# Sums of squares and spread roots of six token blocks as 512-column products, the small tiles' pool opened first, the last output tile in two halves

## The chip, the cores and the metric

The kernel runs on one core of one Trainium2 chip. The core has five engines that run their own instruction streams and wait for one another by semaphores: TensorE (PE in the profile; its weight loads are listed apart as PEld), VectorE (DVE), ScalarE (ACT), GpSimd (POOL) and SyncE (SP), which here issues nearly all DMAs. TensorE writes to PSUM, which has eight banks of 128 x 512 f32; the other tiles lie in SBUF. The metric is the device time of one execution in microseconds (us).

## What is computed

One layer of an encoder on two groups of tokens, 2048 and 512, each with 16 meta tokens in front. All is f32. Cut to what matters here:

```python
u = rms_norm(h, norm_g)                       # h: (tokens, 1024)
qa, ka, va, za, qb, kb, vb, zb, ga, gb = split(u @ w_in)
o_a = neighbourhood_attention(qa, ka, va)     # branch A
o_b = window_attention(qb, kb, vb)            # branch B
y_a = (o_a * silu(za)) @ w_proj_a
y_b = (o_b * silu(zb)) @ w_proj_b
h = h + (sigmoid(ga) * y_a + sigmoid(gb) * y_b) @ w_out
return rms_norm(h[meta tokens dropped], final_g)

def rms_norm(x, g):
    return x * rsqrt(mean(x * x, axis=-1) + 1e-6) * g
```

The two norms need, for every token, a sum of squares over 1024 features, its inverse root, and a multiplication of the token's features by that root.

## The kernel before

Activations lie feature-major: features on the 128 partitions, tokens along the free axis, in blocks (windows) of 512 tokens, numbered 0 to 4. A matrix product in f32 is done as three products of rounded parts: `h` is the value rounded to fp32r by a copy on ScalarE, `l` what is left, by a subtraction (`split`, L198 and L199 for weights); `mm3` (L144 to L146) does `wh*uh`, `wh*ul`, `wl*uh`, each with up to 512 columns.

**A sum of squares** is first added up elementwise over the eight feature tiles into one 128 x 512 tile of partial sums. What is left is a sum over the 128 partitions for each of 512 tokens, and the way back: a tile in which every partition holds the tokens' roots. Before the change, both use plain f32 products with 128-column pieces:

- `sums` (L168): for each of four pieces of 128 tokens, the piece is the stationary operand and a column of ones the moving one. The result is a 128 x 4 tile in PSUM, tokens on the partitions. The trace shows two instructions for each such product.
- `rsqrt` (L151 to L161) computes the inverse root on VectorE in small instructions: a shift and three Newton steps.
- `diagonal` (L175) multiplies `ident` by the roots: four 128 x 128 diagonal matrices side by side, 128 x 512.
- `spread` (L183): `ones` as stationary operand times each diagonal gives 128 x 512 in PSUM with every token's root on all partitions. A copy on ScalarE takes it to SBUF (`rbs` at L1346, `rsa` at L495).

**The order.** TensorE's order is written out by hand throughout, SyncE's in the first part and at the end; the order on the other engines is made by a scheduler that simulates the program with its own durations (`schedule_with_timeline_sim=True`). A group of steps is a generator, and `yield` marks where the next piece of other work goes.

**First part** (0 to about 740 us): projections. `pairs` does the products for two windows at once, 18 pairs of feature tiles with seven series of twelve products each, and calls `step(j, 0)`, `step(j, 1)` and `step(j, 2)` at three places of pair j. There one step of `ahead` runs, if (j, place) is in a list. In the first pass `ahead` is `prep_ahead`, which normalises windows 2 and 3 for the second pass: sixteen steps load x and add up squares (GpSimd, L472); then, at (9, 0), the sums, the roots and the diagonals (L477 on); at (9, 1) the loads of the first piece; at (10, 0) the spread (L495) and the scaling, and so on. The tiles are `x0` of pool `st`, with one buffer.

**Second part** (to about 1825 us): attention units of both branches, in which dense work is filled in: the remaining gate projections, then for each window `dense_pa` (products of branch A with `w_proj_a`, gates loaded into `sga`, L1294 multiplies them into `ta`), `dense_pb`, `dense_out` (products with `w_out`, residual, squares added up in `ssq` by GpSimd, L1336), and `dense_fin`, the final norm of windows 0 to 3. `dense_fin(w - 1)` runs beside `dense_pa(w)`: after every two sub-steps of products, one step of it. It issues sums, roots and the diagonals at its first step, and five steps later the spread, the copy `rbs`, and then eight multiplications of `hT` on GpSimd (L1350) with their stores. Its PSUM tiles come from `ps_d`, which has two banks and also serves the products of `dense_pa`. In this part GpSimd also does the low parts of the weights (L199).

`open_dense` closes the pools `uxp` (operands of window 4, small tiles) and `ev` (evictions) and opens in their memory first `mp` (products' results, `hT`) and then `dn` (small tiles: gate loads `sg` with three buffers, `ssq`, `rbs`, the roots).

**End**: `finish_end` does window 4 token-major: eight output tiles of 128 tokens x 512 features, (b, c) with c = 0 for all b first, 24 products of 512 columns each. Behind each: the residual is added (L1427), the square is summed along the free axis (L1428), and for c = 1 the root of the two sums is computed (L1432, L151 on) and both halves of the row are scaled (L1434, L1436) and stored.

Of the kernel before, what the change touches and what calls it, by code (L numbers as in the profile page):

```python
# [9 lines left out]
F32 = mybir.dt.float32  # L10
# [7 lines left out]
P = 128  # L18
# [77 lines left out]
def encoder_block(ctx: ExitStack, tc: tile.TileContext, xT, x_end, w_in, w_pa, w_pb, w_o, norm_g, final_g,  # L96
# [24 lines left out]

    const = ctx.enter_context(tc.tile_pool(name="const", bufs=1))
# [5 lines left out]
    nc.scalar.activation(warm, ones[:, 0:1], AF.Silu)  # L128
# [4 lines left out]

    def f32(ap):
        return ap.bitcast(F32)
# [28 lines left out]
    def sums(ssq, c0, m, nc_, psum, tag):  # L164

        v = psum.tile([P, WTOK], F32, tag=tag, name="fin_v")
        for c in range(nc_):
            nc.tensor.matmul(v[:m, c : c + 1], ssq[:, c0 + c * m : c0 + (c + 1) * m], ones[:, 0:1],  # L168
                             start=True, stop=True)
        return v[:m, :nc_]  # L170

# [7 lines left out]
    def spread(psum, tag, dg, m, nc_):  # L179

        rb = psum.tile([P, WTOK], F32, tag=tag, name="rs_rb")
        for c in range(nc_):
            nc.tensor.matmul(rb[:, c * P : c * P + m], ones[:m, :], dg[:m, c * m : c * m + m], start=True, stop=True)  # L183
        return rb
# [272 lines left out]
    def prep_ahead(w):  # L457
# [16 lines left out]
        v = ps_t.tile([P, WTOK], F32, tag="vt", name="fin_v")  # L474
        for i in range(2):
            for c in range(4):
                nc.tensor.matmul(v[:, 4 * i + c : 4 * i + c + 1], x0[:, i, c * P : (c + 1) * P], ones[:, 0:1],  # L477
                                 start=True, stop=True)
        r = rsqrt(uxp, v[:, :8], P, 8)
        dgs = [ev.tile([P, WTOK], F32, tag="t", name="rs_dg", bufs=3) for _ in range(2)]  # L480
        for i in range(2):
            diagonal(dgs[i], r[:, 4 * i : 4 * i + 4], P)
        yield
        for kk in range(4):
            x0 = st.tile([P, 4, WTOK], F32, tag="x0", name="xa", bufs=1)
            for half in range(2):
                move(x0[:, 2 * half : 2 * half + 2],
                     xT[(kk + 4 * half) * P : (kk + 4 * half + 1) * P, w * WTOK : (w + 2) * WTOK]
                     .rearrange("p (i t) -> p i t", t=WTOK))
            yield  # L490
            if kk == 0:
                rss = []
                for i in range(2):
                    rss.append(ev.tile([P, WTOK], F32, tag="t", name=f"rsa{i}", bufs=3))
                    nc.scalar.copy(rss[i], spread(ps_t, "vt", dgs[i], P, 4))  # L495
# [12 lines left out]
            move(pre_d[:, kk, 6], t4)  # L508
            yield
# [474 lines left out]
    steps = [(0, 1), *((n, i) for n in range(1, KT) for i in (0, 1)), (KT, 0), (9, 0), (9, 1),  # L984
# [284 lines left out]
    def open_dense():  # L1269
        last.close()  # L1270
        pools["m"] = ctx.enter_context(tc.tile_pool(name="mp", bufs=1, side="right", reuse_waits="tile"))
        pools["d"] = ctx.enter_context(tc.tile_pool(name="dn", bufs=2, side="right", reuse_waits="tile"))
# [83 lines left out]
    def finish_end():  # L1356
# [49 lines left out]
        def out(ps, b, c, ks):  # L1406
            wh, wl = halves[c]
            ts = slice(b * P, (b + 1) * P)
            for k in ks:
                mh, ml = ms[k]  # L1410
                nc.tensor.matmul(ps, mh[:, ts], wh[:, k, :], start=k == 0, stop=False)
                nc.tensor.matmul(ps, mh[:, ts], wl[:, k, :], start=False, stop=False)
                nc.tensor.matmul(ps, ml[:, ts], wh[:, k, :], start=False, stop=k == KT - 1)
# [5 lines left out]
        for c in range(2):  # L1419
            cs = slice(c * WTOK, (c + 1) * WTOK)  # L1420
            for b in range(4):
                ts = slice(b * P, (b + 1) * P)
                h, sq = hs[b], small[:, 4 * b : 4 * b + 3]
                ahead = bool(begun)
                ps = begun.pop(0) if ahead else bank("pse")
                out(ps, b, c, range(KT - 2 if ahead else 0, KT))
                nc.vector.tensor_add(h[:, cs], h[:, cs], ps)  # L1427
                nc.scalar.activation(ps, h[:, cs], AF.Square, accum_out=sq[:, c : c + 1])  # L1428
# [3 lines left out]
                nc.vector.tensor_add(sq[:, 2:3], sq[:, 0:1], sq[:, 1:2])  # L1432
                r = rsqrt(pools["d"], sq[:, 2:3], P, 1)
# [13 lines left out]
    def phases(w, br):  # L1447
# [208 lines left out]
```

## Time and profile before

| | us |
|---|---|
| median of three runs | 1897.26 |
| the three runs | 1896.54 to 1899.39 |
| the profiled execution | 1896.82 |
| its span, first to last instruction | 1894.7 |
| TensorE busy | 1863.0 |
| VectorE busy | 1341.5 |
| ScalarE busy | 1144.3 |
| GpSimd busy | 733.1 |

A row of the order of time reads: start, duration, engine, line, operation, output <- inputs, partitions x elements and types, number of merged instructions, and in brackets the idle time of the engine before it and what ended that. TensorE's products overlap: a row's duration is longer than the step from one start to the next, and it is the step that counts. A row of the waits reads: engine, output, line, what it waited for; us in total, number of times, the longest. A row of the groups ends with total busy time, mean ns of one, and the idle time before. A row of the windows gives the stretch and its length, then busy us and number of instructions of PE, PEld, DVE, ACT and POOL, then the granted clock, the share of the DMA engines, and GB/s. TensorE's granted clock was 0.999 in the mean over the span.

### The profile page before, as it was taken

Reading aid. Unit: us, or ns where it says so; the run is one execution under the profiler, and the core shown is the slowest. Engines: PE = TensorE matmul, PEld = TensorE weight load, DVE = VectorE, ACT = ScalarE, POOL = GpSimd, SP = SyncE. Lnnn points to the kernel's source line nnn. Section 1 sums busy time; section 2 is a strip of 40 time slices with the busy share of each in tenths; the row PEclk is TensorE's granted clock in tenths of the full one; section 3 lists DMA queues with packets and bytes.
Section 4 is the critical chain, followed back from the end, with each engine's and each line's share of the span. In section 5 each row is a group of like instructions: output and inputs, shape, how many; then the busy total and the mean of one; then the engine's idle time right before and its main releaser. Section 6 shows DMA issues by size and latency. Waiting matters only on the chain. (4 is left out here: it accounts for less than half of the span.)

```text
span 1894.7 us, 29723 instructions
## 1 busy us (share of the span) xinstructions
PE 1863.0 (98%) x9797; PEld 1585.1 (84%) x9797; DVE 1341.5 (71%) x2939; ACT 1144.3 (60%) x2523; POOL 733.1 (39%) x556
## 2 busy tenths in 40 slices
PE   8999999999999999999999999999999999999998
PEld 6898888888888888888888888888888888888886
DVE  8886666556477565444457888878888887888874
ACT  6454444444365444444456787897788778778932
POOL 2005442323102232323224336656754864585420
PEclk9999999999999999999999999999999999999999
DMA  7667756644296787644268878967976996697483
GB/s 262 236 177 293 209 173 183 212 172 178 84 354 227 218 222 199 201 135 160 106 218 306 264 230 264 305 201 254 314 246 216 290 313 212 213 315 253 125 289 141
DMA packets 290385, 424.83 MB, mean 224 GB/s; under 512 B 117416, under 2 KB 162040, under 8 KB 288696
## 3 DMA queue, kind: packets, MB, share of 16 engines
q1 hardware_dynamic: 289944, 422.93, 69.2%
q8 instruction: 78, 1.28, 0.3%
q14 instruction: 75, 0.61, 0.1%
q10 hardware_dynamic: 288, 0.01, 0.0%
HBM read 303.46 MB, written 119.39 MB: 223 GB/s over the span
## 5 line engine op out<-in xcount | busy, mean ns | idle before, releaser
L199 POOL TENSOR_TENSOR wt<-wraw,wt 128x512 fp32r<-128x512 f32 x164 | 215.0, 1328 | 283.9 <-ACT wt L198 283.9
L826 PE MATMUL pa<-u,wt 128*128 128x512 f32 x1008 | 242.7, 390 | 0.0
L826 PE MATMUL pa<-u,x 128*128 128x512 f32 x984 | 236.8, 389 | 0.9 <-ACT u L837 0.9
L198 ACT CAST wt<-wraw 128x512 fp32r<-128x512 f32 x312 | 177.7, 619 | 77.0 <-PE mm L146 36.4
L826 PEld LDWEIGHTS pa<-u,wt 128*128 128x128 f32 x1008 | 188.8, 188 | 39.1
L826 PEld LDWEIGHTS pa<-u,x 128*128 128x128 f32 x984 | 184.4, 188 | 40.1 <-ACT u L837 1.7
L797 POOL TENSOR_TENSOR s<-wraw,raw 128x512 f32<-128x512 f32 x40 | 58.3, 1457 | 275.1 <-DVE x L199 275.1
L144 PE MATMUL mm<-u,wt 128*128 128x512 f32 (+2 forms) x416 | 150.8, 362 | 8.0 <-ACT u L325 7.4
L792 POOL TENSOR_TENSOR s<-raw 128x512 f32<-128x512 f32 x40 | 58.4, 1461 | 253.5 <-DMA raw<-in_w_in_dram 250.1
L146 PE MATMUL mm<-u,wt 128*128 128x512 f32 (+2 forms) x416 | 147.1, 354 | 1.9 <-DVE wt L199 1.9
L145 PE MATMUL mm<-u,wt 128*128 128x512 f32 (+2 forms) x416 | 147.0, 353 | 0.7 <-DVE u L326 0.7
L199 DVE TENSOR_TENSOR wt<-wraw,wt 128x512 fp32r<-128x512 f32 x148 | 107.9, 767 | 53.2 <-ACT wt L198 52.8
L826 PE MATMUL pe<-u,wt 128*128 128x512 f32 x504 | 121.3, 390 | 0.0
L826 PE MATMUL pc<-u,wt 128*128 128x512 f32 x504 | 121.1, 389 | 0.0
L826 PE MATMUL pe<-u,x 128*128 128x512 f32 x480 | 115.3, 389 | 0.0
L826 PEld LDWEIGHTS pc<-u,wt 128*128 128x128 f32 x504 | 94.6, 188 | 19.6
L826 PEld LDWEIGHTS pe<-u,wt 128*128 128x128 f32 x504 | 94.5, 188 | 19.6
L1122 DVE TENSOR_TENSOR pl<-tp,ph 128x384 fp32r<-128x384 f32 (+6 forms) x160 | 94.5, 591 | 22.3 <-ACT ph L1121 20.6
L144 PE MATMUL pso<-mh,wt 128*128 128x512 f32 x256 | 107.1, 418 | 0.0
L805 POOL TENSOR_TENSOR s<-wraw,s 128x512 f32<-128x512 f32 x40 | 55.0, 1374 | 131.5 <-DVE wt L199 131.5
L826 PEld LDWEIGHTS pe<-u,x 128*128 128x128 f32 x480 | 90.1, 188 | 18.7
L1027 ACT ACTIVATE prs<-s,nm 128x402 f32<-128x402 f32 (+1 forms) x160 | 91.0, 571 | 20.8 <-DVE nm L1020 17.7
(246 smaller groups left out, 5028.0 us busy)
## 6 DMA issues: line engine op xcount, KB each, us to landing
wraw<-in_w_in_dram SPq DMA_DIRECT2D x86, 512.0 KB
qa<-evq SPq DMA_DIRECT2D x20, 1024.0 KB
raw<-in_w_in_dram SPq DMA_DIRECT2D x40, 512.0 KB
q<-qa SPq DMA_DIRECT2D x20, 1024.0 KB
wraw<-in_w_o_dram SPq DMA_DIRECT2D x32, 512.0 KB
kbt<-kb SPq DMA_DIRECT2D x32, 384.0 KB
qb<-evq SPq DMA_DIRECT2D x20, 512.0 KB
ka<-evk SPq DMA_DIRECT2D x20, 512.0 KB
```

What stands on the lines that cost most here:

```text
L144: nc.tensor.matmul(ps, wh, uh, start=first, stop=False)
L145: nc.tensor.matmul(ps, wh, ul, start=False, stop=False)
L146: nc.tensor.matmul(ps, wl, uh, start=False, stop=last)
L198: nc.scalar.copy(h, r)
L199: low[0] = (eng or lo_eng[0]).tensor_sub(l, r, f32(h)).ins
L792: eng.tensor_add(s1, a21, a22)
L797: eng.tensor_sub(s3, a11, a21)
L805: eng.tensor_sub(s4, a12, s2)
L826: nc.tensor.matmul(ps, wt[:, a, s], u[:, b, kk, :], start=first and kk == 0 and i == 0, stop=kk == 3 and i == 2, skip_group_check=True)
L1027: nc.scalar.activation(out, s, AF.Exp, bias=nm, scale=-1.0, accum_out=sm)
L1122: nc.vector.tensor_sub(pl_[:kb, a], tb, f32(ph_[:kb, a]))
```

## The change

- **Sums** of six token blocks, two in `prep_ahead` and four in `dense_fin`, are done by `sums_parts`: the tile of partial sums is split into two rounded parts, and `ones_r` (128 x 128, now fp32r) as stationary operand times each part, 512 columns, adds up to a 128 x 512 tile in PSUM in which every partition has all sums. Four multiplications of a 128 x 128 piece with `ident`, each with a reduction along the free axis, take out the diagonals: a 128 x 4 tile, as before.
- **The roots** are spread by `spread_parts`: roots are split into two parts, each gets its own diagonals (`diagonal_parts`), and two products of 512 columns add up in PSUM.
- In `prep_ahead` the steps move: the split at (8, 1), the sums and roots at (8, 2), now with four columns for each block instead of eight for both, the spread and the first loads at (9, 1); the diagonals lie in the `x0` buffer.
- In `dense_fin` the split is a step of its own, one step earlier than the sums, whose place in TensorE's order stays. The high part of the sums and of the diagonals use the buffer `rbs`, the low parts one of the three `sg` buffers and `ssq`.
- `open_dense` opens `dn` ahead of `mp`.
- The **last output tile** (3, 1) is done in two halves of 256 columns with a bank each; the residual and square of each half follow it.
- `ones` is made from `ident` by VectorE, and `warm` has its own memset. The two norms at the very beginning (`prep_last`, `prep_first`) keep their products.

```diff
-    ones = const.tile([P, P], F32, name="ones")
-    nc.vector.memset(ones, 1.0)
+    ones_r = const.tile([P, P], F32R, name="ones")
+    nc.vector.tensor_scalar(ones_r, ident, 0.0, 1.0, ALU.mult, ALU.add)
+    ones = f32(ones_r)
...
+    def sums_parts(small, h, l, psum, tag):
+        v = psum.tile([P, WTOK], F32, tag=tag, name="fin_v")
+        nc.tensor.matmul(v, ones_r, h, start=True, stop=False)
+        nc.tensor.matmul(v, ones_r, l, start=False, stop=True)
+        sq = small.tile([P, 8], F32, tag="rq0", name="rq")[:, :4]
+        for c in range(4):
+            piece = v[:, c * P : (c + 1) * P]
+            nc.vector.tensor_tensor_reduce(piece, piece, ident, 1.0, 0.0, ALU.mult, ALU.add, sq[:, c : c + 1])
+        return sq
+
+    def diagonal_parts(small, dh, dl, r):
+        rh, rl = (small.tile([P, 8], F32R, tag=f"rq{i}", name="rq")[:, :4] for i in (1, 2))
+        nc.scalar.copy(rh, r)
+        nc.vector.tensor_sub(rl, r, f32(rh))
+        diagonal(dh, f32(rh), P)
+        diagonal(dl, f32(rl), P)
+
+    def spread_parts(psum, tag, dh, dl):
+        rb = psum.tile([P, WTOK], F32, tag=tag, name="rs_rb")
+        nc.tensor.matmul(rb, ones_r, dh, start=True, stop=False)
+        nc.tensor.matmul(rb, ones_r, dl, start=False, stop=True)
+        return rb
...
     def prep_ahead(w):
...
+        parts = []
         for i in range(2):
-            for c in range(4):
-                nc.tensor.matmul(v[:, 4 * i + c : 4 * i + c + 1], x0[:, i, c * P : (c + 1) * P], ones[:, 0:1],
-                                 start=True, stop=True)
-        r = rsqrt(uxp, v[:, :8], P, 8)
-        dgs = [ev.tile([P, WTOK], F32, tag="t", name="rs_dg", bufs=3) for _ in range(2)]
+            e = ev.tile([P, 2, WTOK], F32R, tag="ev", name="xq")
+            split(e[:, 0, :], e[:, 1, :], x0[:, i])
+            parts.append((e[:, 0, :], e[:, 1, :]))
+        yield
+        dg = st.tile([P, 4, WTOK], F32R, tag="x0", name="rs_dg", bufs=1)
         for i in range(2):
-            diagonal(dgs[i], r[:, 4 * i : 4 * i + 4], P)
+            r = rsqrt(uxp, sums_parts(uxp, *parts[i], ps_t, "vt"), P, 4)
+            diagonal_parts(uxp, dg[:, i], dg[:, 2 + i], r)
         yield
+        rss = []
+        for i in range(2):
+            rss.append(ev.tile([P, WTOK], F32, tag="t", name=f"rsa{i}", bufs=3))
+            nc.scalar.copy(rss[i], spread_parts(ps_t, "vt", dg[:, i], dg[:, 2 + i]))
...
-    steps = [(0, 1), *((n, i) for n in range(1, KT) for i in (0, 1)), (KT, 0), (9, 0), (9, 1),
+    steps = [(0, 1), *((n, i) for n in range(1, KT) for i in (0, 1)), (KT, 0), (KT, 1), (KT, 2), (9, 1),
...
     def dense_fin(w):
-        r = rsqrt(pools["d"], sums(acc["s", w], 0, P, 4, ps_d, "d"), P, 4)
-        dg = pools["d"].tile([P, WTOK], F32, tag="rbs", name="rs_dg", bufs=1)
-        diagonal(dg, r, P)
+        small, ssq = pools["d"], acc["s", w]
+        sh = small.tile([P, WTOK], F32R, tag="rbs", name="ssh", bufs=1)
+        sl = small.tile([P, WTOK], F32R, tag="sg", name="ssl", bufs=3)
+        split(sh, sl, ssq)
+        yield
+        r = rsqrt(small, sums_parts(small, sh, sl, ps_d, "d"), P, 4)
+        dh, dl = (small.tile([P, WTOK], F32R, tag=t, name="rs_dg", bufs=1) for t in ("rbs", "ssq"))
+        diagonal_parts(small, dh, dl, r)
         for _ in range(5):
             yield
-        rb = spread(ps_d, "d", dg, P, 4)
+        rb = spread_parts(ps_d, "d", dh, dl)
...
+                if (b, c) == (3, 1):
+                    for i in range(2):
+                        x = slice(i * 2 * P, (i + 1) * 2 * P)
+                        ps = bank("pse")[:, : 2 * P]
+                        out(ps, b, c, range(KT), x)
+                        residual(ps, h[:, WTOK + x.start : WTOK + x.stop], sq[:, 1 + 2 * i : 2 + 2 * i])
...
-            yield from islice(pa, 3)
+            yield from islice(pa, 2)
             yield from with_fill(pa, dense_fin(w - 1))
```

More of the change, by code (lines that the diff above doesn't have):

```diff
@@ L120, in encoder_block, with f32 @@
     g_d = {(b, w, f): dt(f"g{b}{w}{f}", [P, WTOK]) for b in "ab" for w in range(NWIN) for f in range(KT)}
+    def f32(ap):
+        return ap.bitcast(F32)
     const = ctx.enter_context(tc.tile_pool(name="const", bufs=1))
@@ L162, in rsqrt @@
         return r
[L164 to L168, printed above, removed]
-                             start=True, stop=True)
-        return v[:m, :nc_]
     def diagonal(dg, r, m):
@@ L490, in prep_ahead @@
             yield
[L491 to L495, printed above, removed]
             x = [x0[:, j] for j in range(4)]
@@ L1270, in open_dense @@
         last.close()
-        pools["m"] = ctx.enter_context(tc.tile_pool(name="mp", bufs=1, side="right", reuse_waits="tile"))
-        pools["d"] = ctx.enter_context(tc.tile_pool(name="dn", bufs=2, side="right", reuse_waits="tile"))
+        for i, name, bufs in ("d", "dn", 2), ("m", "mp", 1):
+            pools[i] = ctx.enter_context(tc.tile_pool(name=name, bufs=bufs, side="right", reuse_waits="tile"))
     acc = {}
@@ L1405, in finish_end, with out @@
             move(hs[b], x_end[b * P : (b + 1) * P])
-        def out(ps, b, c, ks):
+        def out(ps, b, c, ks, x=slice(0, WTOK)):
             wh, wl = halves[c]
@@ L1422, in finish_end @@
                 ts = slice(b * P, (b + 1) * P)
-                h, sq = hs[b], small[:, 4 * b : 4 * b + 3]
+                h, sq = hs[b], small[:, 4 * b : 4 * b + 4]
                 ahead = bool(begun)
[L1425 to L1428, printed above, removed]
+                if (b, c) == (3, 1):
[4 more added lines that the diff above has]
+                        residual(ps, h[:, WTOK + x.start : WTOK + x.stop], sq[:, 1 + 2 * i : 2 + 2 * i])
+                        if i == 0:
+                            nc.vector.tensor_add(sq[:, 0:1], sq[:, 0:1], sq[:, 1:2])
+                    sq = sq[:, 0:4:3]
+                else:
+                    ps = begun.pop(0) if ahead else bank("pse")
+                    out(ps, b, c, range(KT - 2 if ahead else 0, KT))
+                    residual(ps, h[:, cs], sq[:, c : c + 1])
                 if c == 0:
@@ L1431, in finish_end @@
                     continue
-                nc.vector.tensor_add(sq[:, 2:3], sq[:, 0:1], sq[:, 1:2])
-                r = rsqrt(pools["d"], sq[:, 2:3], P, 1)
+                nc.vector.tensor_add(sq[:, 0:1], sq[:, 0:1], sq[:, 1:2])
+                r = rsqrt(pools["d"], sq[:, 0:1], P, 1)
                 nc.scalar.mul(h[:, :WTOK], h[:, :WTOK], r)
```

16 lines of the change are left out of this document (8 added, 8 removed).

## Prediction

> **What bounds the kernel now.** I read the page first, then who TensorE waited for, then the order of time around each place that the change touches.
>
> ```profile
> PE 1863.0 (98%) x9797; PEld 1585.1 (84%) x9797; DVE 1341.5 (71%) x2939; ACT 1144.3 (60%) x2523; POOL 733.1 (39%) x556
> PE psa L144 <- ACT rbs L1346: 2.5, 3, 0.9
> ```
>
> TensorE is busy nearly all of the span. So TensorE time that is removed is worth its full length, as long as no other engine is late at that place. The span is 1894.7 us in an execution of 1896.82 us, so 2.1 us lie around it; the median of the three runs is 1897.26 us, 0.44 above the profiled execution. I work against 1896.82.
>
> The second line is the wait that lies where the change does: three of the four blocks in the second half end with TensorE waiting up to 0.9 us for the copy `rbs` on ScalarE. What stands behind this wait decides the change.
>
> ```profile
> 1286.67 0.69 DVE L1294 TENSOR_TENSOR ta<-psa,sga 128x512 f32<-128x512 f32 x1
> 1287.42 0.50 PE L144 MATMUL psa<-ya,wt 128*128 128x512 f32 x1
> 1288.06 2.54 POOL L199 TENSOR_TENSOR wt<-wraw,wt 128x512 fp32r<-128x512 f32 x2 [6.26 <-ACT wt L198]
> 1288.24 1.14 DVE L152 TENSOR_SCALAR rs<-rs 128x4 int32<-128x4 int32 x1
> 1289.42 1.22 DVE L153 TENSOR_SCALAR rs<-rs 128x4 int32<-128x4 int32 x1
> 1295.56 0.68 DVE L175 TENSOR_TENSOR rs_dg<-ident,rs 128x512 f32<-128x512 f32 x1
> 1299.08 2.64 POOL L199 TENSOR_TENSOR wt<-wraw,wt 128x512 fp32r<-128x512 f32 x2 [8.48 <-ACT wt L198]
> 1300.08 1.05 PE L183 MATMUL rs_rb<-rs_dg,ones 128*128 128x128 f32 x8
> 1303.54 0.57 ACT L1346 COPY rbs<-rs_rb 128x512 f32<-128x512 f32 x1
> 1304.17 0.50 PE L144 MATMUL psa<-ya,wt 128*128 128x512 f32 x1 [0.88 <-ACT rbs L1346]
> 1292.00:1297.00 5.00, 5.00 (x34) 4.42 (x33) 4.89 (x19) 3.64 (x10) 0.00 (x0) 1.00 0.85 308
> ```
>
> These are rows in order of time of the first block, and one stretch of the windows (its third busy time is VectorE's). VectorE is full here: 4.89 of 5 us. Two tiny instructions of the root chain took 1.14 and 1.22 us, each until one of GpSimd's pair of subtractions was over. The copy `rbs` starts over 2 us after its products have ended, because ScalarE works through instructions that wait for VectorE. So in this block VectorE leads, and TensorE follows it at the end.
>
> **The change part by part. Products.** The old series of narrow products cost this much (last block; then the two blocks of `prep_ahead`):
>
> ```profile
> 1797.88 0.95 PE L168 MATMUL fin_v<-ones,ssq 128*128 128x1 f32 x8
> 1798.69 0.47 PE L144 MATMUL psa<-ya,wt 128*128 128x512 f32 x1
> 1799.01 0.39 PE L145 MATMUL psa<-ya,wt 128*128 128x512 f32 x1
> 1809.08 1.05 PE L183 MATMUL rs_rb<-rs_dg,ones 128*128 128x128 f32 x8
> 1809.88 0.48 PE L144 MATMUL psa<-ya,wt 128*128 128x512 f32 x1
> 291.67 2.88 PE L826 MATMUL pa<-u,x 128*128 128x512 f32 x12
> 294.39 1.84 PE L477 MATMUL fin_v<-ones,xa 128*128 128x1 f32 x16
> 298.95 2.88 PE L826 MATMUL pc<-u,wt 128*128 128x512 f32 x12
> 315.28 1.95 PE L183 MATMUL rs_rb<-rs_dg,ones 128*128 128x128 f32 x16
> 319.81 2.43 PE L826 MATMUL pc<-u,wt 128*128 128x512 f32 x10
> ```
>
> From 291.67 to 294.39 TensorE does twelve 512-column products: 2.72 us, 0.227 for one. In the last block the sums take 0.81 us up to the next product and that product 0.32 instead of 0.23: 0.90; the spread 0.80, and 0.09 behind it taken alike: 0.89; together 1.79. Four 512-column products take 4 x 0.227 = 0.91. That is 0.88 us of TensorE less in each of four `dense_fin`. In `prep_ahead`, from the sums to the next series but one are 4.56, and from the spread 4.53, each less 2.72: 1.84 + 1.81 = 3.65 for two blocks, against 8 x 0.227 = 1.82. That is 1.83 less. All six: 5.4 us.
>
> **What is added on the other engines.**
>
> ```profile
> L1020 DVE CUSTOM_DVE_ANT_0 s<-s,bb 128x274 f32<-128x274 f32 x32 | 13.8, 452 | 1.6 <-PE s L1201 1.2 <-ACT ph L1121 0.4
> L1020 DVE CUSTOM_DVE_ANT_0 s<-s,ba 128x512 f32<-128x512 f32 x32 | 21.9, 686 | 4.4 <-PE s L1092 4.3
> 300.81 0.17 DVE L159 TENSOR_TENSOR rs<-rs,rs 128x8 f32<-128x8 f32 x1
> ```
>
> A reduction of 128 columns isn't in the trace. The first two rows give 0.98 ns a column, so 0.31 us by their line; it is at most 0.45, with a small instruction of 0.17 to read its accumulator, and no less than such a small one. The last row shows one of these in the root chain; with the gap behind it I count 0.2 us a step. I take 0.3 for a reduction, four to a block: 1.2 us (0.7 to 2.5). A split costs VectorE about 0.69 (as `rs_dg`) and ScalarE about the 0.57 of `rbs`; the low part of the roots a small instruction of 0.17, the copy of the high part about 0.2 on ScalarE, and the second diagonal 0.69. Each block gets 2.7 us more of VectorE and 0.8 of ScalarE. In `dense_fin` the split is issued one step earlier and the rest where it was.
>
> *Blocks 1 to 3.* The split and the four reductions come before the two instructions that stood behind GpSimd until 1290.6 anyway; I count them as hidden by that wait (if GpSimd's pair comes elsewhere, they cost up to 1.8). But `psa` at 1287.42 follows within 0.06 us on the end of `ta` (1286.67 + 0.69), whose bank it takes; so the 0.45 saved on the sums is lost to this wait. Behind 1295.56 come 0.85 us (low part, second diagonal) on a full VectorE, ahead of what ScalarE needs before `rbs`. About half of that fits into VectorE's short idle times. So the wait for `rbs` ends 0.4 us later than now, wherever TensorE stands: +0.4 each, **+1.2** together. Bounds: -1.76 each (0.88 saved and the wait gone) to +2.7 each (all added VectorE time in the way).
>
> *Block 4 and `prep_ahead`.*
>
> ```profile
> 1810.83 7.67 POOL L1350 TENSOR_TENSOR hT<-hT,rbs 128x512 f32<-128x512 f32 x5 [17.76 <-ACT rbs L1346]
> 296.00:301.00 5.00, 5.00 (x25) 4.12 (x25) 4.87 (x11) 1.21 (x2) 2.60 (x2) 1.00 0.11 16
> 1280.53 1.27 POOL L1336 TENSOR_TENSOR ssq<-ssq,xres 128x512 f32<-128x512 f32 x1
> ```
>
> In the last block GpSimd stood idle for 17.8 us before `hT`, which follows on `rbs` less than 1 us after the spread; so nothing holds VectorE up and TensorE leads: **-0.9** (bounds -0.9 to +0.5, the low diagonal late).
>
> In `prep_ahead` the sums move to before the series at 291.67, the spread to before the third series behind the one at 298.95, about 307; so the chain has 14 us. It needs 2 x (1.2 + 13 steps of 0.2 + 0.5 for the copy's round trip + 0.17 + 1.3) = 11.5. VectorE has other work there, about 4.5 us by my estimate, and its window from 296 is full today. The second low diagonal comes about 0.7 us after TensorE asks for it: -1.83 + 0.7 = **-1.1** (-1.83 to +1.7 if all other work goes first). SyncE's loads at that step now wait for the spread too, since the diagonals stand in the loads' buffer; they are queued behind weight loads that wait for buffers, so I count nothing.
>
> *New waits.* The split on ScalarE waits for the last addition to `ssq`, which ends at 1281.8 in block 1, nearly 5 us ahead of the old sums, so the earlier step can have it. The copy of the high roots on ScalarE waits for the end of the root chain; behind it stand the attention units' exponentials, and TensorE's transposes wait for those. It costs nothing while the scheduler puts it late enough, and up to the chain's delay where it doesn't: that is in the bounds of +2.7. The low part of the sums takes one of the three `sg` buffers, so two gate loads go out a tile later; each still has two tiles of twelve products, over 5 us, and the load below took 3.8.
>
> **The pools' order.** The first gate load of the dense part lands late:
>
> ```profile
> 1118.80 0.41 SPq L140 DMA_DIRECT2D gb<-eva  x1
> 1122.09 6.41 SPq L140 DMA_DIRECT2D sga<-ga  x5
> 1125.93 0.69 DVE L1294 TENSOR_TENSOR ta<-psa,sga 128x512 f32<-128x512 f32 x1 [1.14 <-DMA sga<-ga]
> 1126.68 0.50 PE L144 MATMUL psa<-ya,wt 128*128 128x512 f32 x1 [0.57 <-DVE ta L1294]
> ```
>
> Now `dn` stands in memory that the evictions of the last gates used, so its first load can't start before `gb<-eva` has left; after the change it stands where the last window's operands were, free once the last gate's products are done. If the load goes 1 us earlier TensorE gets 0.57 back: **-0.6** (0 if SyncE's queue held it).
>
> **The last tile.**
>
> ```profile
> 64.93 0.28 PE L144 MATMUL mm<-u,wt 128*128 128x256 f32 x1
> 65.77 0.28 PE L145 MATMUL mm<-u,wt 128*128 128x256 f32 x1
> L1228 DVE TENSOR_TENSOR pl<-tp,ph 128x256 fp32r<-128x256 f32 x64 | 26.5, 414 | 0.0
> 1886.69 0.69 DVE L1427 TENSOR_TENSOR h<-h,pse 128x512 f32<-128x512 f32 x1 [1.04 <-PE pse L1413]
> 1887.47 0.60 ACT L1428 ACTIVATE pse<-h 128x512 f32<-128x512 f32 x1 [1.85 <-DVE h L1427]
> ```
>
> The first two are seven steps apart: 0.12 us for a 256-column product, so 48 x 0.12 = 5.76 against 24 x 0.227 = 5.44: +0.32 on the path. The tail is shorter by 0.11 (last product 0.28 instead of 0.39), 0.28 (addition 0.41 instead of 0.69) and about 0.22 (the square of 0.60, cut alike): **-0.3** in all. The first half's addition and square lie beside the second half's products. `ones` made from `ident` costs a fraction of a microsecond at a time when all engines still wait for the first loads: nothing.
>
> **Sum.** +1.2 - 0.9 - 1.1 - 0.6 - 0.3 = -1.7 us: 1895.1 on the profiled execution, **1895.5** beside the median.
>
> [...] One more row pair shows what the added instructions can meet:
>
> ```profile
> 298.57 1.30 POOL L793 TENSOR_TENSOR s<-s,wraw 128x512 f32<-128x512 f32 x1
> 298.76 1.14 DVE L159 TENSOR_TENSOR rs<-rs,rs 128x8 f32<-128x8 f32 x1
> ```
>
> An instruction of VectorE with two operands in SBUF, 0.17 us at 300.81, ended only when GpSimd's did. [...]
>
> **Rivals.**
>
> *All of it lands* (0.30). If the scheduler, which orders VectorE and ScalarE by its own simulated times, puts `rbs` ahead of the attention work, or the 0.85 us fit, nothing is given back: -(4 x 0.88 + 1.83 + 0.6 + 0.3) = -6.3, so 1891, and 1888.5 if the 2.5 us of waits for `rbs` go too. For it: TensorE is the bound at 98%. Against it: VectorE's 4.89 of 5 us.
>
> *The second diagonal meets GpSimd* (0.10; slower). The place is the pair of subtractions at 1299.08. The first diagonal now ends at 1296.2; with 0.85 us and the copy's round trip the second ends at 1297.5 to 1299. If it starts after 1299.08 it stands behind up to 2.64 us, the spread with it, and the maxima of the next attention units too; TensorE waits some 2.0 us more per block than now: 3 x 2.0, nothing won in block 4, +1.0 in `prep_ahead`, -0.9 for the rest: +6, so 1903. It decides from a chain that is 1.5 us longer than I take it.
>
> *The products are not cheaper* (0.05). If a 512-column product with the rounded `ones` cost as much as its four old pieces, only VectorE's work would be new: +1.2 + 0.4 + 0.7 - 0.9, so 1898.5.
>
> **How the numbers follow.** Forecast 0.55, between 1893 and 1898.5. About 0.2% (3.8 us) is what a measurement of this kernel can tell from no change. The case where all lands is over that line, with a small part of the forecast: faster 0.33. Slower 0.10, the second rival. Same 0.57. The range goes from 1889.5, most of the first rival, to 1900.5, which leaves out the second.
>
> **What would show it.** Right: `fin_v` and `rs_rb` with two products each, 0.45 us apart from the next; the wait for `rbs` still there in three blocks at about 1.3 us; none in the fourth; `sga` landing before `ta` asks; the tail from the last product to the end some 0.6 us shorter. Wrong: TensorE waiting for `rs_dg` in `dense_fin`, or the waits for `rbs` gone. What would overturn the sum is another order of VectorE's instructions over the whole second half, since the scheduler sees new durations.

## The result and the profile after

The change makes the kernel slower: median 1911.87 us, against 1898.41 us of the kernel before in all its runs up to then. The ratio is 1.0068, with a 95% interval from 1.0053 to 1.0083, so about 13 us. One of the six runs of the changed kernel took 5480.28 us, and one of the kernel before in a later batch 5386.77; ratios and intervals leave such runs out, and without it the median here is 1911.05. The prediction was 1895.5, in a range from 1889.5 to 1900.5.

The page of the changed kernel (its profiled execution took 1915.09 us, 4 us more than that median), then the waits of TensorE (engine and line, what it waited for, total, times, longest):

```profile
span 1912.9 us, 29727 instructions
PE 1874.3 (98%) x9749; PEld 1582.2 (83%) x9749; DVE 1355.1 (71%) x3021; ACT 1148.4 (60%) x2537; POOL 734.0 (38%) x556
```

```profile
PE tp L1140 <- DVE pr L1060: 5.4, 5, 2.4
PE rs_rb L204 <- DVE rs_dg L169: 5.2, 4, 1.7
PE rs_rb L205 <- DVE rs_dg L169: 2.4, 3, 1.1
PE psa L146 <- DVE ta L1316: 1.6, 3, 0.8
```

TensorE is busy for 11.3 us *more* than before (1863.0), though 5.4 us of its work were taken away. The waits on the new spreads (`rs_rb` for `rs_dg`) are 7.6 us; the 2.5 for `rbs` are gone. So waiting is not the whole story: something makes TensorE's own work longer. In the order of time, a stretch of the first part that the change doesn't touch:

```profile
618.55 2.88 PE L848 MATMUL pc<-u,wt 128*128 128x512 f32 x12
621.27 2.97 PE L848 MATMUL pa<-u,x 128*128 128x512 f32 x12
624.08 2.97 PE L848 MATMUL pe<-u,x 128*128 128x512 f32 x12
626.89 2.89 PE L848 MATMUL pa<-u,wt 128*128 128x512 f32 x12
629.62 2.88 PE L848 MATMUL pe<-u,wt 128*128 128x512 f32 x12
```

From start to start, the series at 618.55 and 626.89 take 2.72 and 2.73 us, as before. The two between them take 2.81: 0.234 us a product instead of 0.227. Of the seven series of a pair, these are the only two whose moving operand is `u[5]` or `u[6]`, the two operands that lie in the pool `uxp`.

The second place is `prep_ahead`'s spread, with a stretch of the windows behind it (after the six pairs of busy time and count: granted clock, DMA share, GB/s):

```profile
307.31 0.40 PE L204 MATMUL rs_rb<-rs_dg,ones 128*128 128x512 f32 x1
308.78 0.69 DVE L169 TENSOR_TENSOR rs_dg<-ident,rq 128x512 fp32r<-128x512 f32 x1
309.61 0.48 PE L204 MATMUL rs_rb<-rs_dg,ones 128*128 128x512 f32 x1 [1.68 <-DVE rs_dg L169]
309.99 0.68 DVE L169 TENSOR_TENSOR rs_dg<-ident,rq 128x512 fp32r<-128x512 f32 x1
310.72 0.50 PE L205 MATMUL rs_rb<-rs_dg,ones 128*128 128x512 f32 x1 [0.63 <-DVE rs_dg L169]
311.00:315.00 4.00, 4.00 (x12) 3.09 (x12) 1.47 (x3) 0.58 (x1) 1.66 (x1) 0.57 0.41 151
```

TensorE waits 2.3 us for the second block's diagonals. After that it is granted 0.57 of its clock for 4 us: the 12 products that start at 311.06 take 4.34 us up to the next series instead of 2.72. The granted clock is 0.50 from 311.43 to 314.84 us, so of these 3.41 us 1.7 are lost. Two more such stretches of 3.41 us follow: from 1536.82 us, behind a wait of 2.39 us for `pr`, and from 1826.95 us, behind the last `dense_fin`. In the profiled execution of the kernel before, the clock is 0.50 from 1890.94 us alone, behind the last product.

The third place is each `dense_fin`; the first block:

```profile
1296.94 0.40 PE L186 MATMUL fin_v<-ssl,ones 128*128 128x512 f32 x1
1298.16 0.50 PE L146 MATMUL psa<-ya,wt 128*128 128x512 f32 x1 [0.82 <-DVE ta L1316]
1308.57 3.08 POOL L221 TENSOR_TENSOR wt<-wraw,wt 128x512 fp32r<-128x512 f32 x2 [7.52 <-issue]
1309.07 1.45 DVE L1060 TENSOR_SCALAR pr<-pr,rd 128x384 f32<-128x384 f32 x1
1310.44 1.76 DVE L169 TENSOR_TENSOR rs_dg<-ident,rq 128x512 fp32r<-128x512 f32 x1
1312.25 0.50 PE L205 MATMUL rs_rb<-rs_dg,ones 128*128 128x512 f32 x1 [1.07 <-DVE rs_dg L169]
1313.32 0.57 ACT L1373 COPY rbs<-rs_rb 128x512 f32<-128x512 f32 x1
```

The sums are cheap, and TensorE then waits 0.82 us for `ta`. Ten microseconds later the second diagonal falls beside GpSimd's pair of subtractions (1308.57 to 1311.65) and takes 1.76 us instead of 0.69; TensorE waits for it. In the other blocks it is not the second diagonal. First the second block, then the last:

```profile
1480.41 2.65 POOL L221 TENSOR_TENSOR wt<-wraw,wt 128x512 fp32r<-128x512 f32 x2 [8.65 <-issue]
1481.85 1.23 DVE L197 TENSOR_TENSOR rq<-rs,rq 128x4 fp32r<-128x4 f32 x1
1483.73 0.50 PE L204 MATMUL rs_rb<-rs_dg,ones 128*128 128x512 f32 x1 [1.11 <-DVE rs_dg L169]
1825.24 0.49 PE L204 MATMUL rs_rb<-rs_dg,ones 128*128 128x512 f32 x1 [1.35 <-DVE rs_dg L169]
1826.45 0.50 PE L205 MATMUL rs_rb<-rs_dg,ones 128*128 128x512 f32 x1 [0.72 <-DVE rs_dg L169]
```

In the second block, and alike in the third, the low part of the roots (L197), which takes 0.16 us in the last block, lies beside GpSimd's pair and takes 1.23, so both diagonals come late. In the last block GpSimd stands still (19.87 us idle up to 1827.65); there the chain alone is too long. From the first reduction (1814.25) to the end of the high diagonal (1825.19) it takes 10.9 us with other work of VectorE in between; before the change, the roots and the diagonal took 6.0.

### The profile page after: what moved, and what is told of

Read it like the earlier page. It is cut to its first block, busy times and chain, and to the rows that moved or that the text cites. A ratio compares the mean times of both kernels' runs of the same rounds, so it can differ in the third digit from the quotient of the medians.

```text
span 1912.9 us, 29727 instructions
## 1 busy us (share of the span) xinstructions
PE 1874.3 (98%) x9749; PEld 1582.2 (83%) x9749; DVE 1355.1 (71%) x3021; ACT 1148.4 (60%) x2537; POOL 734.0 (38%) x556
## 5 line engine op out<-in xcount | busy, mean ns | idle before, releaser
L1143 ACT CAST ph<-tp 128x384 fp32r<-128x384 f32 (+6 forms) x160 | 81.2, 508 | 38.4 <-PE tp L1140 37.1
```

The source lines that it names most:

```text
L1143: nc.scalar.copy(ph_[:kb, a], tb)
```

## The experiments

Three theories: **place** (the new small tiles moved `u5` and `u6` in memory), **waits** (late diagonals, and the halved clock behind them), **order** (another order of VectorE, ScalarE and loads everywhere). Each time stands beside the median of the kernel before in the same batch of runs.

### Where the operands lie

e1, the kernel before with dead bytes, at the start of `prep_ahead`:

```diff
+        uxp.tile([P, 24], F32, tag="pad", name="pad")
```

> The kernel before, with nothing but 96 dead bytes per partition in the pool uxp, which moves u5, u6, u45 and u46 by the 96 bytes by which the change moves them. Theory 'place': a 512-column product takes 0.234 us instead of 0.227 when its moving operand and the weights that are loaded beside it start at different places within 128 bytes; 1008 products (pa, pe, pb and pg from x) would go from 0.227 to 0.234: about +7.1 us, up to +8.5 with the gates' products, so 1905 to 1907, and the series pa<-u,x at 2.81 us for twelve every second time. Theory 'order': the slower series of the changed kernel come from its other order of VectorE, ScalarE and the loads; then the padding alone changes nothing: 1898 and 2.72 us for twelve everywhere.

Measured: 1904.42 (before 1897.69; ratio 1.0037, 1.0025 to 1.0049): 6.7 us for 96 unused bytes.

```profile
500.78 2.97 PE L827 MATMUL pe<-u,x 128*128 128x512 f32 x12
503.59 2.89 PE L827 MATMUL pa<-u,wt 128*128 128x512 f32 x12
L827 PE MATMUL pe<-u,x 128*128 128x512 f32 x148 | 36.8, 396 | 0.0
```

Its instructions stand in the same order as before the change on every engine, and the series with `u6` takes 2.81 us (last row: the group between 330 and 640 us, with its mean of 396 ns). Place is shown; order falls for this part.

e2 moves the weights by 32 bytes as well; e3 is the changed kernel with 32 dead bytes more in `uxp` and 64 in `dn`:

```diff
     const = ctx.enter_context(tc.tile_pool(name="const", bufs=1))
+    const.tile([P, 8], F32, name="pad")            # e2, with e1's line
...
+        uxp.tile([P, 8], F32, tag="pad", name="pad")   # e3
...
+        pools["d"].tile([P, 16], F32, tag="pad", name="pad", bufs=1)   # e3
```

> The kernel before with those 96 bytes in uxp and 32 more in const, so that every operand of the first part, moving or weight, starts at a multiple of 128 bytes instead of 96 bytes behind one. If it is the difference of the two places that counts, the first part is back at 0.227 us a product and only the last output tiles (weights at 96, moving operand at 0) are slower, 0.233 for about 190 products: 1898 to 1900. If a start at a multiple of 128 is slow in itself, all 3500 products of the first part take 0.234: about +24 us, 1922. Theory 'order': 1898.

> The changed kernel with 32 dead bytes in uxp and 64 in dn, so that u5, u6, mh and ml start where they did before the change, within 128 bytes. 'Place': 1008 products get 0.007 us back, the gates' a little, and the 168 of the last output tiles 0.006 each: 7.1 + 1.1, so about -8 to -9 us, 1903 to 1904; what is left above the kernel before, some 5 us, is the waits for rs_dg and the halved clock behind them. 'Order': 1912, unchanged.

Measured: e2 1904.68 (1.0035, 1.0022 to 1.0048), e3 1909.46 (1.0069, 1.0054 to 1.0084). e2 misses all that was expected: the products with `u5` and `u6` are still slow, those with `u[0]` to `u[4]` fast, though all start at a multiple of 128. e3 brings next to nothing, as theory 'order' had it, but for another reason: its products with `u5` and `u6` are still slow too. From the start addresses in the built programs and the mean steps between starts of products (those under 0.26 us):

```
kernel        u5 starts at   weights x at   distance mod 256   step, u5 or u6 with x
before        190176         151008           0                0.227 us
changed, e1   190080         151008         160                0.234
e2            190080         151040         128                0.233
e3            190048         151008         128                0.233
f1 (below)    189920         151008           0                0.227
```

So in these kernels the step goes with the distance between the moving operand and the weights that are loaded beside it: 0.227 us where the last column but one is 0, 0.233 to 0.234 where it is 128 or 160. f1 moves `u5` and `u6` by 256 bytes against the kernel before:

```diff
+        uxp.tile([P, 40], F32, tag="pad", name="pad")
...
+        pools["d"].tile([P, 16], F32, tag="pad", name="pad", bufs=1)
```

> The changed kernel with 160 dead bytes in uxp and 64 in dn: u5, u6, u45 and u46 lie 256 bytes below where they lay before the change, so every moving operand and the weights loaded beside it start alike within 256 bytes, where the kernel with 32 dead bytes left them 128 apart. Theory 'place within 256': all products of the first part at 0.227 again, 1008 x 0.006 plus some 690 opening products x 0.004, so 7 to 8 us under the realigned kernel (1909.5): 1901 to 1903. Rival: the distance counts within 512 bytes or more, or the right-hand pool must lie exactly where it did; then 0.233 stays and the time is 1908 to 1910.

Measured: 1905.21 (before 1897.31; 1.0039, 1.0027 to 1.0051).

```profile
499.23 2.88 PE L849 MATMUL pe<-u,x 128*128 128x512 f32 x12
501.95 2.88 PE L849 MATMUL pa<-u,wt 128*128 128x512 f32 x12
L849 PE MATMUL pe<-u,x 128*128 128x512 f32 x158 | 38.1, 389 | 0.0
```

The products of the first part have their old step: the series at 499.23 takes 2.72 us, and one of `pe<-u,x` lasts 389 ns on the mean (last row, groups between 330 and 640 us), 396 in e1. The changed kernel stood 12.6 us over its runs of before (by the median of 1911.05), f1 7.9: 4.7 us by place here, with a margin of some 4 us, and 6.7 in e1. The two traces are sharper: f1's instructions stand in the same order as those of the changed kernel on every engine, and from 320 to 980 us the changed kernel falls 6.8 us behind it, step by step. The median is 2 to 4 us above what was expected, so more than the rest of the first part is left.

### Which of the parts costs the rest

e4 is the changed kernel with `prep_ahead` and its steps as before (`uxp` keeps its size by that) and 64 dead bytes in `dn`:

```diff
...
-    steps = [..., (KT, 0), (KT, 1), (KT, 2), (9, 1),
+    steps = [..., (KT, 0), (9, 0), (9, 1),
...
```

> The changed kernel with prep_ahead as before (its narrow products, one root for both blocks), so that uxp keeps its size, and 64 dead bytes in dn. Only dense_fin, the pools' order and the last tile differ from the kernel before. If the two waits for rs_dg at 309 us (1.7 and 0.6) and the halved clock behind them (3.4 us at half speed, so 1.7) cost 4.0 and the cheaper products give 1.8 back, this is 2 us faster than the realigned kernel: 1901 to 1902. If the second halves of the waits are hidden anyway, it is 1.8 slower than that: 1905.

Measured: 1898.26 (before 1897.69; 1.0002, 0.9994 to 1.0011). That is 7.3 us under f1, each beside its own runs of before; f1 differs in `prep_ahead` alone, and the distance is far more than the 2.3 us of its waits. (By the intervals given, a distance between two versions has a margin of 2 to 4 us.) And `dense_fin`, the pools and the tail together can't be told from nothing.

f2, f3 and f4 were to put the spread one step later, f3 in `dense_fin` too; f4 has the old `dense_fin`:

```diff
-    steps = [..., (KT, 0), (KT, 1), (KT, 2), (9, 1),
+    steps = [..., (KT, 0), (KT, 1), (9, 0), (9, 1),
...
-        for _ in range(5):      # f3, dense_fin
+        for _ in range(6):
```

> The same, and in prep_ahead the spread (and the loads behind it) one step later, where the loads stood before the change. Theory 'late diagonals': the waits for rs_dg at 309 us (1.7 + 0.6) go, and with them the 3.4 us at half clock behind them (1.7): about 4 us under the first of these, 1897 to 1899. Rival 'the scheduler moves it all back': VectorE's and ScalarE's instructions of the chain are issued later in the same measure and TensorE waits as long as before: 0.

> The same as f2, and in dense_fin the spread one step later too (six steps between diagonal and spread instead of five). Theory 'the low diagonal meets GpSimd and is late': the four waits for rs_dg (1.1 + 1.2 + 1.2 + 2.1 in the changed kernel) go, 5.5 us; where the copy rbs on ScalarE is then waited for again (0.9 in three blocks before), 3 are left: 3 to 5.5 us under f2, 1892 to 1895. Rival: rbs comes a step later too, hT with it, and the wait only changes its name: 0 to -1.

> f2 with dense_fin as before the change: narrow products, one diagonal, no split. It holds prep_ahead's products, the pools' order and the halved last tile alone. Expected against the kernel before: -1.8 for prep_ahead, -1.0 for the pools' order (the waits for ta and y at 1119 us gone), -0.5 at the tail, so 1894 to 1895. If dense_fin as changed is a loss (waits for rs_dg of 5.5 and for ta of 1.7, against 3.5 of products and 2.5 of old waits), this is 1 to 2 us under f2; if the two are even, 0.

Measured, against 1897.31: f2 1908.11 (1.0061, 1.0048 to 1.0074), f3 1915.06 (1.0093, 1.008 to 1.0106), f4 1904.4 (1.0038, 1.0026 to 1.005). All expectations missed, because the edit did something else: step (9, 0) runs the *sums*, so they came one series later and the spread stayed. That is the opposite test, and a clear one (f4):

```profile
307.63 0.40 PE L213 MATMUL rs_rb<-rs_dg,ones 128*128 128x512 f32 x1
313.18 0.76 PE L212 MATMUL rs_rb<-rs_dg,ones 128*128 128x512 f32 x1 [5.15 <-DVE rs_dg L169]
316.00:320.00 4.00, 4.00 (x14) 3.15 (x13) 0.00 (x0) 0.76 (x2) 0.00 (x0) 0.68 0.97 323
```

One series less between sums and spread (2.72 us) makes TensorE wait 2.9 us longer, and the clock is 0.81 from 305 to 316 us and 0.68 from 316 to 320: some 6.8 us at half clock, from 1.5 us before the wait is over if they lie in one piece. f4, with the old `dense_fin`, is 3.7 us under f2: beside late diagonals in `prep_ahead` the new `dense_fin` is a loss, which e4 alone doesn't show. f3 also shows that a later spread in `dense_fin` is no remedy: it is 7 us over f2.

g1 is f1 with the spread where it was meant to go; g2 is e4 with one fp32 diagonal and four narrow products in `dense_fin` (and 192 dead bytes in `dn`); g3 is the kernel before with the pools' order and the halved last tile alone, g4 the same with g1's `prep_ahead`:

```diff
-    steps = [..., (KT, 0), (KT, 1), (KT, 2), (9, 1),
+    steps = [..., (KT, 0), (KT, 1), (KT, 2), (9, 2),     # g1, g4
...
-        dh, dl = (small.tile([P, WTOK], F32R, tag=t, name="rs_dg", bufs=1) for t in ("rbs", "ssq"))
-        diagonal_parts(small, dh, dl, r)
+        dg = small.tile([P, WTOK], F32, tag="rbs", name="rs_dg", bufs=1)     # g2
+        diagonal(dg, r, P)
...
-        rb = spread_parts(ps_d, "d", dh, dl)
+        rb = spread(ps_d, "d", dg, P, 4)
```

> f1 (the changed kernel, placed as before within 256 bytes) with the spread and the loads behind it two series later in prep_ahead: seven series between sums and spread, where the change has five and the kernel before eight. In f2 and f3 the step that I moved held the sums, not the spread: they left only four series there, and TensorE waited 5.2 us instead of 1.7 + 0.6. Theory 'too few series between sums and spread': two series are 5.4 us, more than the 2.3 that TensorE waits in f1, so no wait for rs_dg near 310 us, no halved clock behind it, and 2.3 to 4 us under f1 (1905.2): 1901 to 1903; the rest of the distance to 1898 lies in the second half. Rival 'the chain is put off by the other work, whatever its distance': the waits stay, 1905.

> The kernel with prep_ahead as before (1898.3), where dense_fin keeps the new sums but spreads with one fp32 diagonal and four narrow products per block as before: no low part of the roots, no second diagonal. Theory 'the second diagonal on VectorE is what TensorE waits for': the waits for rs_dg (3.6 + 1.8 us) go, 0.44 x 4 = 1.8 us of products come back, and of the old waits for rbs (2.5) about half return: 1 to 3 us less, 1895 to 1897. Rival 'the whole chain is late': rs_dg is waited for all the same and the products come back on top: 1900.

> The kernel before with the pools' order and the halved last tile alone (and ones made from ident). The first gate load of the dense part leaves before ta asks: -0.6 to -1.0 near 1120 us (before: 0.6 for ta and 0.4 for y); the tail from the last product to the end is 0.6 shorter and the halves cost 0.3 more: -0.3. Together -1, 1896.5; a rival is that another load is late in its place (kd at 1006 us: 1.5 us in the changed kernel, 0.3 before): +0.5.

> g3 with prep_ahead's new products too, the spread seven series behind the sums as in g1. If nothing waits, 1.8 us under g3: 1894.5 to 1895, the fastest of all. If the added work of VectorE and ScalarE shifts the series around it: as g3 or up to 2 above.

Measured, against 1897.6: g1 1897.9 (1.0005, 0.9996 to 1.0015), g2 1895.13 (0.9991, 0.9982 to 1.0001), g3 1895.92 (0.9994, 0.9984 to 1.0003), g4 1896.59 (0.9998, 0.9989 to 1.0007). In g1 the spread waits for nothing:

```profile
308.85 2.89 PE L849 MATMUL pe<-u,wt 128*128 128x512 f32 x12
311.58 0.39 PE L204 MATMUL rs_rb<-rs_dg,ones 128*128 128x512 f32 x1
312.28 0.39 PE L205 MATMUL rs_rb<-rs_dg,ones 128*128 128x512 f32 x1
318.00 2.88 PE L849 MATMUL pc<-u,wt 128*128 128x512 f32 x12
```

The series `pc` starts at 318.00, before the change at 319.81: the products' saving is there in full at that place. The first row of the waits of e4, then two of g2's and one of g4's, all in the second part:

```profile
PE rs_rb L204 <- DVE rs_dg L169: 3.6, 3, 1.4
```

```profile
PE psa L146 <- ACT rbs L1374: 2.9, 2, 1.6
PE rs_rb L177 <- DVE rs_dg L169: 0.2, 1, 0.2
```

```profile
PE s L1122 <- DMA kd<-kam: 1.1, 1, 1.1
```

With one diagonal (and without the low part of the roots, which goes with it), the wait for `rs_dg` is down to 0.2 and the one for `rbs` is back at 2.9: g2 is 3.0 us under e4 when each is taken beside its own runs of before, which is hardly more than the margin. g3 and g4 can't be told apart, nor from the kernel before: each interval is some 3.5 us wide, as much as the parts are worth together. So the 1.8 us of `prep_ahead` don't show in a time: g1 isn't under e4, nor g4 under g3, nor h1 (below) under g2. In g1's trace TensorE waits 1.5 us for `u` at 720 us and 1.8 for `kd` at 1005, where the kernel before waits 0.9 and 0.3. One loss stands in both traces: at the start of the attention work TensorE waits for the load of `kd`, 1.1 us in g4 and 1.2 in g3, 0.3 before the change. It is 0.5 to 1.8 in every version with the new order of the pools but f3, and at most 0.3 in e1, e2 and f3; why wasn't tried.

### Is it the wait, or the place of the spread?

h2 is f1 with one root chain for both blocks, the spread where the change has it; h3 is f1 with g2's `dense_fin`; h1 is g1 with g2's `dense_fin`:

```diff
...
-        for i in range(2):
-            r = rsqrt(uxp, sums_parts(uxp, *parts[i], ps_t, "vt"), P, 4)
-            diagonal_parts(uxp, dg[:, i], dg[:, 2 + i], r)
+        sq = uxp.tile([P, 8], F32, tag="rq0", name="rq")     # h2: both blocks' sums
...
+        r = rsqrt(uxp, sq, P, 8)
+        for i in range(2):
+            diagonal_parts(uxp, dg[:, i], dg[:, 2 + i], r[:, 4 * i : 4 * i + 4])
```

> All parts of the change, corrected: operands placed as before within 256 bytes, the spread of prep_ahead seven series behind the sums, one fp32 diagonal and four narrow products in dense_fin, the pools' order, the halved last tile. By the parts: g2 stands 2.5 us under the kernel before, prep_ahead's products bring 1.8 more where nothing waits: 1893 to 1894. If the parts don't add up because the second half's waits decide, as g2: 1895 to 1896.

> f1 with one root chain for both blocks of prep_ahead instead of two (13 steps of 0.2 us less on VectorE), the spread where the change has it, five series behind the sums. Theory 'the wait for the second diagonals is the cause': the chain is at least 2.6 us shorter, the wait of 2.3 us near 310 us goes or falls under 0.7, and the time falls to 1897 to 1899, like g1. Rival 'it is the place of the spread, the loads or the copies behind it': the wait goes, the time stays at 1903 to 1905.

> f1 with dense_fin as in g2 (one diagonal). Against g2 (1895.1) it has only prep_ahead's part with its wait of 2.3 us. Theory 'the wait costs itself and the halved clock behind it, no more': -1.8 + 2.3 + up to 1.7, so 0.5 to 2.2 above g2: 1895.6 to 1897.5. Theory 'it shifts the second half against something and costs 7 whatever dense_fin does': 1902.

Measured, against 1897.6: h1 1895.52 (0.9992, 0.9983 to 1.0000), h2 1898.54 (1.0009, 1.0000 to 1.0018), h3 1898.98 (1.001, 1.0001 to 1.0019). The four products of h2's spread:

```profile
307.65 0.39 PE L204 MATMUL rs_rb<-rs_dg,ones 128*128 128x512 f32 x1
307.88 0.40 PE L205 MATMUL rs_rb<-rs_dg,ones 128*128 128x512 f32 x1
308.12 0.39 PE L204 MATMUL rs_rb<-rs_dg,ones 128*128 128x512 f32 x1
308.35 0.39 PE L205 MATMUL rs_rb<-rs_dg,ones 128*128 128x512 f32 x1
```

No wait, with the spread where the change has it, and the time is g1's, 7.0 us under f1: the wait is the cause, not the place. h3 has it again (1.7 and 0.6) and stands 3.9 us over g2 and 3.5 over h1. A wait of 2.3 and the 1.7 that a stretch of 3.41 us at half clock cost the changed kernel make 4.0. I had expected 0.5 to 2.2 over g2, with 1.8 off for the products; that saving isn't seen here. In f1 the same wait cost 7.3 to 7.6 (against e4 and g1). The 3.5 us beyond need the late diagonals of the second half too. f1's profiled execution was granted 0.997 of the clock in the mean, g1's 0.998, and in f1 one wait of TensorE for `pr` behind a late gate load is 3.1 us long. The order of instructions isn't the reason: from 333 us on it is the same in f1 and e4 on all engines, SyncE's loads included. Yet in these two traces f1, 2.6 us behind at 317 us and 0.6 at 1006, loses 6 us more between 1515 and 1533, at that wait and behind it, and another 1.5 at the last block. f1, e3 and the changed kernel, with one order, spread such waits differently too. What differs is when a load lands and where half clock follows (in the changed kernel from 311.43 us, in f1 not between 300 and 320 us, where the clock was 1.00); what ties that to 310 us stays open.

## Why the prediction was wrong

**Left out: where the tiles lie.** My sum has terms for instructions, waits and transfers. Three small tiles in `uxp` moved `u5` and `u6` by 96 bytes, and 1008 products paid 7 ns each, so 7 us: 6.7 by the time of e1, 6.8 by the traces of f1 and the changed kernel, half of the loss. The sum put this at nothing without a reason. No view of the kernel before shows it; the new tags and the pool's layout were in the diff.

**Mis-sized: `prep_ahead`.** The step was "The second low diagonal comes about 0.7 us after TensorE asks for it". Measured: TensorE waits 2.3. The 0.7 doesn't come out of the working: a chain of 11.5 us and 4.5 of other work in 14 us are 2.0 late against the start of the spread, whose fourth product comes 0.7 later. And "VectorE has other work there, about 4.5 us by my estimate" was too little: in the changed kernel, ten instructions of other work stand between the first reduction and the last diagonal, from 293.53 to 309.38, 6.9 us:

```profile
293.32 0.29 DVE L190 CUSTOM_DVE_ANT_0 fin_v<-fin_v,ident 128x128 f32<-128x128 f32 x1
293.53 0.14 DVE L190 DVE_READ_ACCUMULATOR2_ANT rq<- 128x1 f32 x1
293.53 0.68 DVE L221 TENSOR_TENSOR wt<-s,wt 128x512 fp32r<-128x512 f32 x1
309.38 0.68 DVE L294 TENSOR_TENSOR tkv<-pe,u 128x512 f32<-128x512 f32 x1
```

A reduction costs 0.29 and its read 0.14, about 0.39 a step where I took 0.3. And I priced the wait at its own length. The runs priced it at 3.5 to 7.6 us, of which the clock explains up to 1.7. The four stretches of half clock in the changed kernel's trace start at 311.43, 1536.82, 1826.95 and (behind its last product) 1908.87 us, so 359, 85 and 24 times 3.413 us apart, and the first three last 3.41 us each. The waits of 1.68 and 0.63 us, with products between, had such a stretch behind them in the changed kernel; in f1 the same pair of 1.6 and 0.6 had none. Why f1's had none, no run shows.

**Wrong wait, and too small a chance: `dense_fin`.** That the saving of the sums is lost to `ta` was right (waits of 0.8, 0.4 and 0.4). That the wait for `rbs` would stay and end 0.4 later was wrong: it went, and a wait of 1.1 us for `rs_dg` in each block took its place. In the first block that is the second diagonal beside GpSimd's pair, the rival to which I gave 0.10; in the next two it is the low part of the roots, which the prediction counts at 0.17, with no wait. "So nothing holds VectorE up and TensorE leads" failed in the last block: GpSimd held nothing up, but the chain was too long, and TensorE waited 2.1 us, with 3.41 us at half clock behind it, where I had -0.9. By e4 the whole of it, with pools and tail, is +0.6 (-1.1 to +2.1), where my sum had -0.6.

**Right.** The products: -1.8 for `prep_ahead` at its place in the trace of g1, though no time shows it. The tail: the last product starts 7.87 us before the end instead of 8.47, 0.6 shorter:

```profile
1905.06 0.28 PE L1440 MATMUL pse<-woh,ml 128*128 128x256 f32 x1
1905.37 0.42 DVE L1443 TENSOR_TENSOR h<-h,pse 128x256 f32<-128x256 f32 x1 [0.50 <-PE pse L1440]
1905.89 0.39 ACT L1444 ACTIVATE pse<-h 128x256 f32<-128x256 f32 x1 [1.04 <-DVE h L1443]
```

The pools' order: no wait for `ta` or `y` is left at the start of the dense part, -1.0. But `kd`, some 110 us ahead of it, is waited for 1.5 us instead of 0.3, so little is left of it.

## What to carry to other kernels

Before a sum is trusted, compare the start addresses of matmul operands in the two built programs: here 96 bytes of new small tiles shifted two large ones and cost 6.7 us (e1). In this kernel, with TensorE busy for 98% of the span, a wait of 2.3 us on a serial chain cost 3.5 to 7.6 us, so leave the chain a series more than it needs, and put fewer instructions on a full engine rather than faster products behind it. Of all versions tried, the best (g2, h1) are about 2 us under the kernel before, at the edge of what the runs can tell: their intervals end at 1.0001 and 1.0000.

## What the hardware showed that was not expected

- In the six kernels of the table a 512-column product of `u5` or `u6` with x steps 0.227 us where its moving operand and the weights loaded beside it start a multiple of 256 bytes apart (the kernel before, f1), and 0.233 to 0.234 us where they start 128 or 160 bytes beyond one. The last output tiles agree: the change moved `mh` and `ml` (there the weights) from 0 to 192 bytes beyond such a multiple, and 0.227 became 0.233. The products `pso` do not follow: they step 0.230 us on the mean at a distance of 0 (before) as at 64 (changed kernel).
- Waits of 1.68 and 0.63 us at 310 us had 3.41 us at half clock behind them in the changed kernel, and the same pair had none in f1, where the clock was 1.00 from 300 to 320 us. With a wait of 5.22 us f2 had 0.81 of the clock from 307 to 313 us and 0.67 from 313 to 320, and with one of 5.15 f4 had 0.81 from 305 to 316 and 0.68 from 316 to 320: some 6.8 us at half clock in both. None followed the single waits of 1.1 us in the first three blocks of the changed kernel, and e4's clock was 1.00 in all four parts of 1100 to 1830 us.
- In the two traces of the kernels before and after, what tells the stretches' beginnings apart is the idle time of TensorE in the 3.413 us ahead. Counted behind 50 us in steps of 3.413 us from the stretches' own starts, the three steps ahead of a stretch in the changed kernel have 2.22, 2.18 and 2.06 us of it, and no other step at full clock up to the last product has over 1.31. In the kernel before, no step up to the last product was followed by half clock, and none has over 1.83. A wait of 2.18 us at 58 us in the changed kernel falls into two steps, of 1.23 and 1.22 us idle, and no half clock followed.
